# One attention layer's instruction order: a block of queries projected between the first scores, TensorE held to the written order, turned keys in two pairs and a single

## The chip, the cores and the metric

The kernel runs on one core of one Trainium2 chip. The metric is the device time of one execution in microseconds (us), as the median of several runs. A core has a matrix engine (TensorE, PE in the profile), a vector engine (VectorE, DVE), a scalar engine (ScalarE, ACT), GpSimd (POOL) and SyncE (SP), which here only issues DMAs. Each engine works through its own list of instructions in order and waits on semaphores for the others.

## The reference, cut to what matters

The program is a two-layer trunk over 512 latent tokens and 256 context tokens of width 1024. Layer 0 mixes tokens with a chunkwise mLSTM, layer 1 with windowed attention, and each layer ends with a squared-ReLU MLP. Only layer 1's attention is touched. Its core is, with 16 query heads in 4 groups of 4, one key/value head for each group, head width 64, blocks of 128 queries, a window of 128 and one sink logit for each head:

```python
rel = k_idx - SWA_BLOCK - q_idx
def block(args):
    j, qb = args                       # one block of 128 queries
    kb = lax.dynamic_slice_in_dim(kp, j * SWA_BLOCK, 3 * SWA_BLOCK, axis=1)   # its own block and both neighbours
    ...
    m = jnp.maximum(jnp.maximum(jnp.max(s_lat, -1), jnp.max(s_ctx, -1)), sink_g)
    p_lat = jnp.exp(s_lat - m[..., None])
    p_ctx = jnp.exp(s_ctx - m[..., None])
    den = jnp.sum(p_lat, -1) + jnp.sum(p_ctx, -1) + jnp.exp(sink_g - m)
    o = jnp.einsum("bhgqk,bkhd->bqhgd", p_lat, vb) + jnp.einsum("bhgqc,bchd->bqhgd", p_ctx, cv)
    return o / jnp.moveaxis(den, 3, 1)[..., None]
```

Before it stand the projections of queries, keys and values (queries and keys are rotated, "rope"), behind it an output projection of 1024 by 1024 that is added to the latent stream. In layer 1, the last one, only the latent tokens need an output.

## The kernel before, in words

**Numbers in two halves.** Most operands are held as a high half and a low half (`whi`, `wlo`, `uH`, `uL`), so that one product takes three matmuls (`mm3`, line 107). A weight comes in through `unit_begin` (line 88): a DMA on SP into `raw`, a copy to `whi` on ACT (L95), and, when its returned `end()` is called, a subtraction to `wlo` on DVE (L98). `prefetch` begins a unit and puts its `end()` into a list that `tick()` counts down, one tick for each command of the order tables.

**Names in the profile.** `pk`, `pq`, `pv` are the projections of keys, queries and values (L115, TensorE); `rt`/`rtx`, `rx` are the rotated queries or keys (L1905 to L1907); `ks` and `qs` are keys and queries stacked as high and low half (L1916 on ACT, L1917 on DVE); `s` are the scores of one head for one block of queries (L1956/L1957, or L1960/L1961); `e` are their exponentials; `pt` the transposed (turned) exponentials; `ph` the copy of `pt`; `av` the weighted values; `mm<-y` the output projection; `vst` the values.

**Scores.** `scores(g, j)` (L1932) makes the four heads of group g for query block j, and yields after each one. Blocks j=0 and j=3, at the edge, see two blocks of keys and the context, 512 columns in all, so two heads share one tile `s` of 1024 columns: head 0 with head 1 and head 2 with head 3. Their scores are two matmuls of 512 columns. Blocks j=1 and j=2 see three blocks of keys, 640 columns: one tile for each head, four matmuls. There are two such tiles. After the matmuls, one custom DVE instruction (L1964, with a read of its accumulator) adds the mask and finds the minimum, ACT takes the exponential (L1968) and the sink's (L1971), and after each second head DVE forms the reciprocal of the denominator (L1975, L1976) and POOL scales both heads (L1978). In a shared tile the second head's first matmul carries a semaphore wait on ACT, for the exponential of the first head.

**Weighing.** `weigh` (L1982) gives two lists of steps: T, "turn" (four transposes L1994, one key block of the four heads, and the copy `ph` on ACT, L1999), and V, `values` (the product with the values, L2011/L2017, and the evacuation L2019/L2022). j=0 and j=3 have 4 T steps, j=1 and j=2 have 5.

**The order.** There are 16 turns, n = 4g + j. Each turn walks through the string PAT: S is the scores of one head (running six heads ahead), T one turn step, V one values step, F one filler step. Fillers are queries of a later group (`q_steps`: 8 steps of three 512-column matmuls, then the rotation) in the turns that `qat` names, and parts of the output projection of an earlier group (`out_steps`: two steps of three 512-column matmuls for each part, then an evacuation `hL` on DVE, L1867) in the counts that `outs` names. The last turn, n=15, uses the string PL. Before turn 0 a prologue makes the first six heads' scores with the value projections of key blocks 2 and 3 as fillers (`v_steps`, four steps of six 256-column `pv` matmuls for each block): one S, then two F, six times. `need` says at which turn a weight's DMA is begun.

**Who decides in the end.** The kernel is compiled by a scheduler that may move an instruction past others on its engine. An instruction wrapped in `keep_in_program_order` keeps its place among others so wrapped. `self.matmul` (L113) wraps its matmul when `pin_mm` is set; in before it is not set in this layer, and `scores` and `weigh` call `nc.tensor.matmul` directly.

Of the kernel before, what the change touches and what calls it, by code (L numbers as in the profile page):

```python
# [14 lines left out]
AX = mybir.AxisListType  # L15


PAT = "SFTTFSFTFSTFTFSFFVVV"
PL = "FTTFVTFTFFVFF"
PSUM = bass.MemoryType.PSUM  # L20

P = 128
# [34 lines left out]
class Trunk:  # L57
# [1593 lines left out]
    def layer1_mix(self, u):  # L1651
        nc, tc, a = self.nc, self.tc, self.a
        self.ctx_ada.close()
        with tc.tile_pool(name="sw", bufs=1, reuse_waits="tile") as sw:
# [34 lines left out]
            for m in range(2):  # L1689
# [6 lines left out]
                    self.keys_out(0, rk[0](), slice(0, NL))  # L1696
                self.queries_out(sw, 0, m, rq)

            def v_steps(j, pool, tag):
                ps = pool.tile([P, 512], F32, name="pv", tag=tag)[:, :256]  # L1700
                for i in range(0, KT, 2):
                    self.values(ps, j, rows, i, i + 2)
                    if i < KT - 2:
                        yield
                put(j, ps)
                yield
            for j in range(2):
                for _ in v_steps(j, *((self.mm, "mm"), (self.at, "at"))[j]):
                    pass
            self.ctx_mm.close()  # L1710
            with tc.tile_pool(name="sc", bufs=2, space=PSUM, reuse_waits="tile") as sc, \
                    tc.tile_pool(name="pt1", bufs=3, space=PSUM, reuse_waits="tile") as pt, \
# [1 line left out]
                ys = [None] * KVH  # L1714
                todo = [(g, j) for g in range(KVH) for j in range(4)]
                parts = []
                qat = {0: (1, 0), 1: (1, 1), 2: (2, 0), 3: (2, 1), 4: (3, 0), 8: (3, 1)}
                outs = {5: 3, 6: 3, 7: 2, 9: 3, 10: 2, 11: 2, 12: 2, 13: 3, 14: 6, 15: 6}
                late, soon, units, yh = [], [], {}, {}
                need = {0: "q10", 1: "q11", 2: "q20", 3: "q21", 4: "q30", 5: "o00", 6: "o01", 8: "q31", 9: "o10", 10: "o11",  # L1720
                        12: "o20", 14: "o21 o30", 15: "o31"}
                self.units, self.yh = units, yh

                def prefetch(n, d):
# [40 lines left out]
                    for n, (g, j) in enumerate(todo):  # L1765
                        yield from self.scores(sw, g, j, sc, curs[n])
                sg = all_scores()
                fl = chain(v_steps(2, pt, "pt"), v_steps(3, pt, "pt"))
                for i in range(6):
                    next(sg)  # L1770
                    tick()
                    if i == 1:
                        prefetch(0, 2)
                    next(fl, None)
                    next(fl, None)
                for n, (g, j) in enumerate(todo):
                    if ys[g] is None:
                        ys[g] = sw.tile([P, 2, NL], F32, name=f"yT{g}", tag="yT", bufs=2)
                    if j == 0 and g:
                        parts += self.out_part(g - 1, ys, pt, "pt")  # L1780
                    if n == 14:
                        y3 = self.split_y(3)
                        st3 = {"y": y3}
                        self.st = {}
                        self.tmpA = [self.base.tile([P, NL], F32, name=f"nA{t}", tag=t) for t in ("uH5", "uL5", "uL4")]
                        pa = self.out_part(3, ys, pt, "pt", "A", st3)
                        parts = [f for i in range(4) for f in (parts[i], pa[i])] + pa[4:5]
                        self.split_half(ys[3], y3, 0)
                    if j == 0 and g:
                        yh[g - 1] = self.split_y(g - 1, ys)  # L1790
                    fl = filler(n)
                    wg = self.weigh(sw, g, j, curs[n], pt, av, ys)
                    for i, cmd in enumerate(PAT if n < 15 else PL):
                        next({"S": sg, "F": fl}.get(cmd) or wg[cmd], None)
                        tick()
                        if i == 6:
                            prefetch(n + 1, 7)
                    for it in (wg["T"], wg["V"], fl):
                        for _ in it:
                            pass  # L1800
                self.split_half(ys[3], y3, 1)
                for f in pa[5:]:
                    for _ in f():
# [23 lines left out]
    def split_y(self, g, ys=None):  # L1827

        nc = self.nc
        r = []  # L1830
        for i in range(2):
            hi, lo = [self.base.tile([P, NL], F32R, name=f"y{n}{g}{i}",
                                     tag=f"u{'HL'[n]}{(g - 2) * 6 + i}" if g > 1 else f"uC{2 * i + n}") for n in range(2)]
            if ys:
                nc.scalar.copy(out=hi, in_=ys[g][:, i, :])
                nc.vector.tensor_tensor(out=lo, in0=ys[g][:, i, :], in1=hi.bitcast(F32), op=ALU.subtract)
            r.append((hi, lo))
        return r
# [93 lines left out]
    def scores(self, sw, g, j, scp, out):  # L1932

        nc = self.nc
        d = self.swd
        mm = nc.tensor.matmul
        q4 = d["qs"][g][:, :, j * P:(j + 1) * P]
        k0, k1 = [d["ks"][:, i, g, :] for i in range(2)]
        lo, hi = max(0, j - 1), min(4, j + 2)
# [42 lines left out]
    def weigh(self, sw, g, j, ps_, ptp, avp, ys):  # L1982

        nc = self.nc
        d = self.swd
        mm = nc.tensor.matmul
        blks = list(range(max(0, j - 1), min(4, j + 2))) + [4, 5]
        pq = []

        def turn():  # L1990
            for n, kb in enumerate(blks):
                pt = ptp.tile([P, 512], F32, name="pt", tag="pt")
                for i in range(4):
                    nc.tensor.transpose(out=pt[:, i * P:(i + 1) * P], in_=ps_[i][:, n * P:(n + 1) * P],  # L1994
                                        identity=self.ident)
                self.nph = (getattr(self, "nph", 0) + 1) % 6
                pool, tag = (self.base, f"uC{4 + self.nph}") if self.nph < 4 else (sw, f"ph{self.nph}")
                ph = pool.tile([P, 512], F32, name="ph", tag=tag)
# [176 lines left out]
```

## Time and profile before

| quantity | value |
|---|---|
| median of 3 runs | 1493.35 us (1492.82 to 1493.48) |
| the profiled execution's own time | 1492.53 us |
| its span | 1490.8 us (so 1.73 us lie around it) |
| mean granted TensorE clock | 0.995 of full |
| keys and first queries of layer 1's attention | from 912.9 us |
| first score | 943.00 us |
| last weighted value | 1135.6 us |
| end of its output projection | 1141.8 us |

The profile is one execution. Start times are counted from the start of the span. A row of the timeline gives the start, the busy time, the engine, the source line, the operation, output from inputs, the shape and the count; in brackets stands the idle time ahead of it on that engine and what ended it. Matmuls are pipelined, so a matmul's cost in a dense stretch is the distance from its start to the start of the next one, not its busy time.

### The profile page before, as it was taken

Reading aid. Unit: us, or ns where it says so; the run is one execution under the profiler, and the core shown is the slowest. Engines: PE = TensorE matmul, PEld = TensorE weight load, DVE = VectorE, ACT = ScalarE, POOL = GpSimd, SP = SyncE. Lnnn points to the kernel's source line nnn. Section 1 sums busy time; section 2 is a strip of 40 time slices with the busy share of each in tenths; the row PEclk is TensorE's granted clock in tenths of the full one; section 3 lists DMA queues with packets and bytes.
Section 4 is the critical chain, followed back from the end, with each engine's and each line's share of the span. In section 5 each row is a group of like instructions: output and inputs, shape, how many; then the busy total and the mean of one; then the engine's idle time right before and its main releaser. Section 6 shows DMA issues by size and latency. Waiting matters only on the chain.

```text
span 1490.8 us, 22747 instructions
## 1 busy us (share of the span) xinstructions
PE 1470.4 (99%) x8600; PEld 1299.2 (87%) x8601; DVE 1102.8 (74%) x1996; ACT 740.1 (50%) x1492; POOL 291.5 (20%) x289
## 2 busy tenths in 40 slices
PE   9999999999999999999999999899999999999998
PEld 5888999989899999999999998776767988888886
DVE  4987648488897878788777767667777775857697
ACT  4555353553754241432414344677775655455454
POOL 0123131333103223212223121133332000000000
PEclk9999999999999999999999999999999999999999
DMA  9223313235132334343343422221111432240221
GB/s 374 86 95 123 124 57 125 93 114 166 44 113 85 133 117 146 114 155 130 126 156 100 154 71 89 68 65 57 50 43 61 180 128 98 89 138 33 95 71 57
DMA packets 49317, 161.14 MB, mean 108 GB/s; under 512 B 5776, under 2 KB 8592, under 8 KB 49080
## 3 DMA queue, kind: packets, MB, share of 16 engines
q1 hardware_dynamic: 48032, 157.92, 30.8%
q10 hardware_dynamic: 1175, 1.77, 0.3%
q8 instruction: 68, 1.11, 0.3%
q14 instruction: 42, 0.34, 0.1%
HBM read 153.90 MB, written 2.10 MB: 105 GB/s over the span
## 4 chain that ended last, share of the span: by engine, by line
PE 89%; DVE 6%; ACT 3%; issue 1%; POOL 0%; DMA 0%; POOLq 0%; ACTq 0%; DVEq 0%
PE mm L115 53%; PE p L115 10%; PE pq L115 3%; PE kept L115 3%; PE av L2011 2%; PE pt L1994 2%; PE pb L115 2%; PE pc L115 2%; PE acc L115 1%; PE at L1009 1%; PE s L1960 1%; PE at L966 1%; PE pk L115 1%; PE arow L115 1%; PE s L1961 1%
## 5 line engine op out<-in xcount | busy, mean ns | idle before, releaser
L115 PE MATMUL mm<-h,whi 128*128 128x384 f32 x1024 | 262.4, 337 | 0.0
L1054 DVE TENSOR_TENSOR wlo<-raw,whi 128x1024 fp32r<-128x1024 f32 (+2 forms) x138 | 165.2, 1201 | 74.4 <-ACT whi L1053 72.1
L1053 ACT CAST whi<-raw 128x1024 fp32r<-128x1024 f32 (+2 forms) x138 | 136.0, 991 | 141.0 <-PE mm L115 90.3
L115 PE MATMUL mm<-uH,whi 128*128 128x512 f32 (+1 forms) x496 | 186.6, 380 | 0.0
L115 PE MATMUL mm<-uH,wlo 128*128 128x512 f32 (+1 forms) x496 | 186.6, 377 | 0.0
L115 PE MATMUL mm<-uL,whi 128*128 128x512 f32 (+1 forms) x496 | 186.2, 377 | 0.0
L115 PEld LDWEIGHTS mm<-h,whi 128*128 128x128 f32 x1024 | 185.5, 188 | 0.3 <-DVE h L1054 0.2
L115 PE MATMUL mm<-h,wlo 128*128 128x384 f32 x512 | 172.0, 336 | 0.0
L282 DVE SCALAR_TENSOR_TENSOR adap<-raw,crow 128x1024 bf16<-128x1024 f32 x128 | 165.3, 1292 | 8.3 <-DMA raw<-ada 7.4
L115 PE MATMUL p<-t,whi 128*128 128x384 f32 x448 | 114.3, 336 | 0.0
L1053 ACT CAST whi<-sum 128x512 fp32r<-128x512 f32 (+1 forms) x42 | 31.8, 759 | 159.3 <-PE mm L115 81.1
L115 PEld LDWEIGHTS mm<-uH,wlo 128*128 128x128 f32 x496 | 93.4, 188 | 17.4 <-issue 0.2
L115 PEld LDWEIGHTS mm<-uL,whi 128*128 128x128 f32 x496 | 93.6, 189 | 15.4 <-DVE uL L1099 0.3
L115 PEld LDWEIGHTS mm<-uH,whi 128*128 128x128 f32 x496 | 92.7, 189 | 15.7 <-issue 0.2
L115 PEld LDWEIGHTS mm<-h,wlo 128*128 128x128 f32 x512 | 96.1, 188 | 0.0
L1054 DVE TENSOR_TENSOR wlo<-wb,whi 128x1024 fp32r<-128x1024 f32 x49 | 59.2, 1224 | 35.9 <-ACT whi L1053 35.8
L1054 DVE TENSOR_TENSOR h<-r,h 128x384 fp32r<-128x384 f32 (+2 forms) x100 | 58.2, 584 | 34.2 <-ACT h L1053 33.9
L115 PEld LDWEIGHTS p<-t,whi 128*128 128x128 f32 x448 | 81.2, 188 | 0.0
L1053 ACT CAST whi<-wb 128x1024 fp32r<-128x1024 f32 x49 | 51.5, 1052 | 57.8 <-PE mm L115 48.2
L1978 POOL TENSOR_SCALAR e<-e,den 128x512 f32<-128x512 f32 (+1 forms) x64 | 53.5, 848 | 130.3 <-DVE den L1976 98.9
L115 PE MATMUL mm<-uC,whi 128*128 128x256 f32 x416 | 77.0, 285 | 0.3 <-ACT whi L1053 0.3
L115 PE MATMUL p<-t,wlo 128*128 128x384 f32 x224 | 75.4, 337 | 0.0
(417 smaller groups left out, 3528.4 us busy)
## 6 DMA issues: line engine op xcount, KB each, us to landing
raw<-ada SPq DMA_DIRECT2D x80, 512.0 KB, 3.4
raw<-w SPq DMA_DIRECT2D x64, 512.0 KB, 3.4
raw<-w2a SPq DMA_DIRECT2D x32, 512.0 KB, 3.2
wb<-w2b SPq DMA_DIRECT2D x28, 512.0 KB, 4.1
adaw<-ada SPq DMA_DIRECT2D x16, 512.0 KB, 11.2
raw<-wqk SPq DMA_DIRECT2D x8, 512.0 KB, 4.6
raw<-wv SPq DMA_DIRECT2D x8, 512.0 KB, 3.3
raw<-wo SPq DMA_DIRECT2D x8, 512.0 KB, 3.2
```

Source lines behind the costliest of these rows:

```text
L115: i = self.nc.tensor.matmul(**kw)
L282: self.tc.keep_in_program_order(nc.vector.scalar_tensor_tensor(out=pr, in0=w, scalar=0.5, in1=self.crow[:, v, :], op0=ALU.mult, op1=ALU.mu ...
L966: mm(out=kv[d][64 * h:64 * h + 64, n * VW:(n + 1) * VW], lhsT=kp[:, d, j, 64 * h:64 * h + 64], rhs=v[:, j, h, :], start=True, stop=True)
L1009: mm(out=o[hh][:, i * VW:(i + 1) * VW], lhsT=pw[g, d, hh][:, i, :], rhs=v[:, 3 * g + i, hh, :], start=False, stop=i == 2)
L1053: keep(self.nc.scalar.copy(out=hi, in_=src))
L1054: keep((eng or self.nc.vector).tensor_tensor(out=lo, in0=src, in1=hi.bitcast(F32), op=ALU.subtract))
L1960: mm(out=o, lhsT=ql, rhs=k0[:, cs], start=True, stop=False)
L1961: mm(out=o, lhsT=ql, rhs=k1[:, cs], start=False, stop=True)
L1978: nc.gpsimd.tensor_scalar(out=out[ii][:, :W], in0=out[ii][:, :W], scalar1=den[:, ii:ii + 1], scalar2=1.0, op0=ALU.mult, op1=ALU.mult)
L1994: nc.tensor.transpose(out=pt[:, i * P:(i + 1) * P], in_=ps_[i][:, n * P:(n + 1) * P], identity=self.ident)
L2011: mm(out=o[i * DH:(i + 1) * DH, :], lhsT=v(n + i), rhs=pq[n + i], start=n == 0, stop=n == len(blks) - 2)
```

## The change

Five edits, all in layer 1's attention.

1. The first weight block of group 1's queries (`q10`) is begun before the value projections and split into halves after the first of them; its projection becomes a filler of the prologue. The blocks after it move up by one turn in `qat`: (1,1) in turn 0, (2,0) in 1, (2,1) in 2, (3,0) in 3, (3,1) in 4; turn 8 has none any more.
2. The prologue follows a new string PS: `SSFFSSFFFFSFFFSFFFFF`.
3. `pin_mm` is set from the prologue to the end of turn 15, `scores` and `weigh` call `self.matmul`, and the transposes are wrapped, so TensorE keeps the written order.
4. PAT has the T steps as pair, pair, single. Turns 5 to 12 use a new string PO with four F steps, and `outs` is evened out to two parts in each.
5. `split_y` puts the halves of y of groups 1 and 2 into other tiles; `need` moves the output weights' DMAs.

```diff
-PAT = "SFTTFSFTFSTFTFSFFVVV"
+PAT = "SFTTFSFFSFTTFSTFFVVV"
+PO = "STTFSFSTTFSTFVVV"
+PS = "SSFFSSFFFFSFFFSFFFFF"
 PL = "FTTFVTFTFFVFF"
...
+            first = self.unit_begin(a["wsq"][1, 0])
...
             for j in range(2):
                 for _ in v_steps(j, *((self.mm, "mm"), (self.at, "at"))[j]):
                     pass
+                if j == 0:
+                    first[2]()
...
-                qat = {0: (1, 0), 1: (1, 1), 2: (2, 0), 3: (2, 1), 4: (3, 0), 8: (3, 1)}
-                outs = {5: 3, 6: 3, 7: 2, 9: 3, 10: 2, 11: 2, 12: 2, 13: 3, 14: 6, 15: 6}
-                late, soon, units, yh = [], [], {}, {}
...
+                qat = {0: (1, 1), 1: (2, 0), 2: (2, 1), 3: (3, 0), 4: (3, 1)}
+                outs = {**{n: 2 for n in range(5, 13)}, 13: 4, 14: 6, 15: 6}
+                late, soon, units, yh = [], [], {"q10": first}, {}
...
-                fl = chain(v_steps(2, pt, "pt"), v_steps(3, pt, "pt"))
-                for i in range(6):
-                    next(sg)
+                fl = chain(v_steps(2, pt, "pt"), v_steps(3, pt, "pt"), q_steps(1, 0))
+                self.pin_mm = True
+                for i, cmd in enumerate(PS):
+                    next(sg if cmd == "S" else fl, None)
                     tick()
-                    if i == 1:
-                        prefetch(0, 2)
-                    next(fl, None)
-                    next(fl, None)
+                    if i == 8:
+                        prefetch(0, 8)
+                for _ in fl:
+                    pass
...
-                    for i, cmd in enumerate(PAT if n < 15 else PL):
+                    for i, cmd in enumerate(PO if 4 < n < 13 else PAT if n < 15 else PL):
...
+                self.pin_mm = False
...
-                                     tag=f"u{'HL'[n]}{(g - 2) * 6 + i}" if g > 1 else f"uC{2 * i + n}") for n in range(2)]
+                                     tag=f"u{'HL'[n]}{(0, 2, 0, 6)[g] + i}" if g else f"uC{2 * i + n}") for n in range(2)]
...
-        mm = nc.tensor.matmul
+        mm = self.matmul
...
-                    nc.tensor.transpose(out=pt[:, i * P:(i + 1) * P], in_=ps_[i][:, n * P:(n + 1) * P],
-                                        identity=self.ident)
+                    self.tc.keep_in_program_order(nc.tensor.transpose(
+                        out=pt[:, i * P:(i + 1) * P], in_=ps_[i][:, n * P:(n + 1) * P], identity=self.ident))
```

Three places show what this moves in the compiled programs. Lines of the changed kernel are two to eight higher, and its matmuls all carry the line of `self.matmul`, L117. What an instruction waits for stands in brackets.

**The first scores, TensorE.** In the program before, `s_9816` is the tile of heads 0 and 1, `s_9864` that of heads 2 and 3, and `pv_9823`, `pv_9871` are the value projections of key blocks 2 and 3:

```order
L115 MATMUL pv_9823<-whi_9353,uL0_9038 128x256
L1956 MATMUL s_9816<-ks_9560,qs_9699 128x512 [waits DVE_49]
L115 MATMUL pv_9823<-whi_9353,uH1_9039 128x256
...
L1957 MATMUL s_9816<-ks_9560,qs_9699 128x512 [waits DMAHW5_49,DMAHW7_49,DMAHW4_49,DMAHW3_49]
L115 MATMUL pv_9823<-whi_9393,uL5_9048 128x256
...
L1956 MATMUL s_9864<-ks_9560,qs_9699 128x512 [waits DVE_49,PE_49]
...
L115 MATMUL pq_9943<-uL0_9038,whi_9848 128x512
L1956 MATMUL s_9816<-ks_9560,qs_9699 128x512 [waits Activation_49]
```

In the changed program the tile of heads 0 and 1 is `s_9822`, that of heads 2 and 3 `s_9852`, and `pv_9839` is the value projection of key block 2:

```order
L117 MATMUL pv_9782<-whi_9393,uL7_9052 128x256
L117 MATMUL s_9822<-ks_9560,qs_9699 128x512 [waits DVE_49]
L117 MATMUL s_9822<-ks_9560,qs_9699 128x512 [waits DMAHW5_49,DMAHW7_49,DMAHW4_49,DMAHW3_49]
L117 MATMUL s_9822<-ks_9560,qs_9699 128x512 [waits Activation_49]
L117 MATMUL pv_9839<-whi_9353,uH0_9037 128x256
...
L117 MATMUL pv_9839<-whi_9353,uL3_9044 128x256
L117 MATMUL s_9852<-ks_9560,qs_9699 128x512 [waits DVE_49,PE_49]
L117 MATMUL s_9852<-ks_9560,qs_9699 128x512
L117 MATMUL s_9852<-ks_9560,qs_9699 128x512 [waits Activation_49]
```

Before, the scheduler put the scores of head 2 and 45 matmuls of the value projections between the scores of heads 0 and 1; now the two heads of a tile stand directly behind each other, with the second one's wait for ACT in between, and the value projections stand behind them.

**The first mask instruction, VectorE.** Before, the last rotation and stacking of group 0's keys and queries (`ks`, `qs`) is followed by the mask instructions (ISA) of heads 0 and 1:

```order
L1907 TENSOR_TENSOR rtx_9738<-rtx_9738 128x512 [waits DVE_49]
L1917 TENSOR_TENSOR ks_9560<-rt_9650,ks_9560 64x512 [waits Activation_49] x2
L1917 TENSOR_TENSOR qs_9699<-rtx_9738,qs_9699 64x512 [waits Activation_49] x2
L1964 ISA s_9816,nb_9814<-s_9816,msk_9552,nsink_9550 128x512 [waits PE_49,Pool_49]
L1964 ISA nb_9814 128x1
```

Now the low half of `q10`'s weight stands ahead of the first mask instruction:

```order
L1915 TENSOR_TENSOR rtx_9738<-rtx_9738 128x512 [waits DVE_49]
L1925 TENSOR_TENSOR ks_9560<-rt_9650,ks_9560 64x512 [waits Activation_49] x2
L1925 TENSOR_TENSOR qs_9699<-rtx_9738,qs_9699 64x512 [waits Activation_49] x2
L100 TENSOR_TENSOR wlo_9753<-raw_9750,whi_9752 128x1024
L1972 ISA s_9822,nb_9820<-s_9822,msk_9552,nsink_9550 128x512 [waits PE_49,Pool_49]
```

One instruction moved in: before, `q10`'s `wlo` stood behind the fifth mask instruction of the prologue.

**Turn 5, TensorE.** The end of the turn before, with the scores of heads of group 1, block 3 (512 columns), turned keys, output projection and weighted values:

```order
L1994 MATMUL pt<-ident,e 128x128 x4
L115 MATMUL mm<-y_10448,whi 128x512
L115 MATMUL mm<-y_10449,whi 128x512
L115 MATMUL mm<-y_10448,wlo 128x512
L2011 MATMUL av<-ph,vst_9561 64x512
L1956 MATMUL s<-ks,qs 128x512
L1957 MATMUL s<-ks,qs 128x512
L2011 MATMUL av<-ph,vst_9562 64x512
```

And the same place now, from the first score of such a pair to the second:

```order
L117 MATMUL s<-ks,qs 128x512 [waits PE_49,Activation_49]
L117 MATMUL s<-ks,qs 128x512
L2002 MATMUL pt<-ident,e 128x128 [waits PE_49]
L2002 MATMUL pt<-ident,e 128x128 x3
L117 MATMUL mm<-y_10489,whi 128x512 [waits DVE_49]
L117 MATMUL mm<-y_10490,whi 128x512
L117 MATMUL mm<-y_10489,wlo 128x512
L117 MATMUL s<-ks,qs 128x512 [waits Activation_49]
```

Before, the scheduler had put the second score in between the weighted values; now it stands ahead of them, behind two turn steps and one filler step, and the weighted values stand together.

More of the change, by code (lines that the diff above doesn't have):

```diff
@@ L1716, in layer1_mix @@
                 parts = []
-                qat = {0: (1, 0), 1: (1, 1), 2: (2, 0), 3: (2, 1), 4: (3, 0), 8: (3, 1)}
-                outs = {5: 3, 6: 3, 7: 2, 9: 3, 10: 2, 11: 2, 12: 2, 13: 3, 14: 6, 15: 6}
-                late, soon, units, yh = [], [], {}, {}
-                need = {0: "q10", 1: "q11", 2: "q20", 3: "q21", 4: "q30", 5: "o00", 6: "o01", 8: "q31", 9: "o10", 10: "o11",
-                        12: "o20", 14: "o21 o30", 15: "o31"}
+                qat = {0: (1, 1), 1: (2, 0), 2: (2, 1), 3: (3, 0), 4: (3, 1)}
+                outs = {**{n: 2 for n in range(5, 13)}, 13: 4, 14: 6, 15: 6}
+                late, soon, units, yh = [], [], {"q10": first}, {}
+                need = {0: "q11", 1: "q20", 2: "q21", 3: "q30", 4: "q31", 5: "o00", 7: "o01", 9: "o10", 11: "o11", 13: "o20",
+                        14: "o21 o30", 15: "o31"}
                 self.units, self.yh = units, yh
@@ L1985, in weigh @@
         d = self.swd
-        mm = nc.tensor.matmul
+        mm = self.matmul
         blks = list(range(max(0, j - 1), min(4, j + 2))) + [4, 5]
```

## The prediction

> **What bounds the kernel now.** I read the page first: the span, the share of each engine, the chain that ended last.
>
> ```profile
> span 1490.8 us, 22747 instructions
> PE 1470.4 (99%) x8600; PEld 1299.2 (87%) x8601; DVE 1102.8 (74%) x1996; ACT 740.1 (50%) x1492; POOL 291.5 (20%) x289
> PE 89%; DVE 6%; ACT 3%; issue 1%; POOL 0%; DMA 0%; POOLq 0%; ACTq 0%; DVEq 0%
> ```
>
> TensorE is the bound. No matmul is taken away, so the change can win only what TensorE loses in this layer, and lose what it adds. Next I asked for windows, and for TensorE's waits from 943 us to 1140 us.
>
> ```profile
> 943.00:968.00 25.00, 20.29 (x110) 16.44 (x111) 15.36 (x34) 14.96 (x38) 5.10 (x6) 0.86 0.15 43
> 990.00:1010.00 20.00, 20.00 (x108) 14.33 (x107) 14.34 (x33) 15.83 (x36) 7.77 (x10) 1.00 0.17 50
> PE s L1960 <- ACT e L1968: 3.7, 2, 1.8
> PE mm L115 <- ACT ph L1999: 0.3, 1, 0.3
> ```
>
> The columns are busy us of PE, PEld, DVE, ACT, POOL, then clock, DMA share and GB/s. The first scores have TensorE idle for 4.7 us and at 0.86 of its clock; the turns behind them are full. So the prologue decides, and in the turns only gaps too small for a busy share. Its TensorE timeline:
>
> ```profile
> 941.35 0.28 PE L115 MATMUL pv<-whi,uL 128*128 128x256 f32 x1
> 943.00 0.50 PE L1956 MATMUL s<-ks,qs 128*128 128x512 f32 x1 [1.37 <-DVE rtx L1905]
> 949.75 0.28 PE L115 MATMUL pv<-whi,uL 128*128 128x256 f32 x1
> 949.87 0.40 PE L115 MATMUL pq<-uH,whi 128*128 128x512 f32 x1
> 950.11 0.40 PE L115 MATMUL pq<-uL,whi 128*128 128x512 f32 x1
> 950.74 0.40 PE L1957 MATMUL s<-ks,qs 128*128 128x512 f32 x1
> 952.97 0.39 PE L1960 MATMUL s<-ks,qs 128*128 128x256 f32 x1 [1.83 <-ACT e L1968]
> 955.42 0.78 PE L1956 MATMUL s<-ks,qs 128*128 128x512 f32 x1
> 958.46 0.58 PE L1960 MATMUL s<-ks,qs 128*128 128x256 f32 x1 [1.83 <-ACT e L1968]
> 961.87 0.48 PE L115 MATMUL pq<-uH,whi 128*128 128x512 f32 x1
> 965.17 0.28 PE L1960 MATMUL s<-ks,qs 128*128 128x256 f32 x1
> 965.76 0.60 PE L1994 MATMUL pt<-ident,e 128*128 128x128 f32 x4
> 966.12 0.48 PE L115 MATMUL pq<-uH,whi 128*128 128x512 f32 x1
> ```
>
> From start to start a 256-column matmul costs 0.12 us (949.75 to 949.87), one of 512 columns 0.23 (949.87 to 950.11), a head of four score matmuls 0.59 (965.17 to 965.76), a turn step of four transposes 0.36 plus what its neighbour pays, which I count as 0.44. Between 941.47 and 961.87 stand 45 `pv`, 3 `pq`, 8 wide score matmuls, 3 heads of four and 8 transposes: 5.4 + 0.7 + 1.8 + 1.8 + 0.9 = 10.6 us of work in 20.4 us. **Before loses 9.8 us here.** Some of it is clock, in windows of 3.4 us:
>
> ```profile
> 941.33:944.74 3.41, 2.04 (x16) 1.00 0.44 118
> 951.57:954.98 3.41, 1.28 (x6) 1.00 0.00 0
> 954.98:958.40 3.42, 1.54 (x4) 0.50 0.00 0
> 958.40:961.80 3.40, 3.34 (x12) 0.50 0.20 57
> ```
>
> Here the columns are PE busy, clock, DMA. A window that was 1.28 or 1.54 busy is followed by one at half clock, a window that was 2.04 busy is not, and after a full one (958.40) the clock is back.
>
> **Part by part. The prologue (edits 1, 2, 3).** What comes before the first score is unchanged on TensorE and VectorE, so that score stays at 943.0, but three `pv` fewer stand ahead (941.1). Its second matmul waits for a DMA of keys, which I put at 943.9. Then, in the written order, TensorE stands at head 1, which waits for head 0's exponential, and all `pv` and `pq` are queued behind it. What that waits for:
>
> ```profile
> 946.35 1.41 DVE L1917 TENSOR_TENSOR qs<-rtx,qs 64x512 fp32r<-64x512 f32 x2
> 947.78 0.76 DVE L1964 CUSTOM_DVE_ANT_0 s<-s,msk,nsink 128x512 f32<-128x512 f32 x1
> 951.29 0.76 DVE L1964 CUSTOM_DVE_ANT_0 s<-s,msk,nsink 128x512 f32<-128x512 f32 x1 [2.69 <-PE s L1957]
> 952.14 0.69 ACT L1968 ACTIVATE e<-s,nb 128x512 f32<-128x512 f32 x1 [1.34 <-DVE nb L1964]
> 958.90 1.21 DVE L98 TENSOR_TENSOR wlo<-raw,whi 128x1024 fp32r<-128x1024 f32 x1
> ```
>
> VectorE rotates and stacks until 947.76, then makes `q10`'s `wlo`, 1.21 us, to 948.97, and only then masks. From a mask's start to the score behind its exponential it is 951.29 to 952.97, 1.68 us. So head 1 starts at 950.65. TensorE stood from 944.3: **6.3 us in one piece**; before it filled this with the 45 `pv`.
>
> By the windows, 944.74 to 948.15 is empty and 948.15 to 951.57 a quarter full, so it is half clock until 954.98. There head 1 and twelve `pv` cost 2 x 0.46 + 2 x 1.44 = 3.8 us: to 954.5, then head 2 (0.8, partly at half clock) to 955.3. From head 2's second matmul, about 954.9, to the next score of its tile is 950.74 to 952.97, 2.23 us: head 3 at 957.1, idle 1.8 us. Behind it stand 24 `pv`, a head, 12 `pv`, 3 `pq`, a head, 21 `pq`, with no wait that I can see. Losses: 1.9 ahead of the first score, 0.7 inside it, 6.3, half clock 2.4, then 1.8 = 13.1 to 13.2 us. **Against 9.8: +3.4 us.** Bounds: without half clock the 2.4 shrink, and the wait for head 2 moves up, to +1.5; if the window 954.98 to 958.40, which I get at about half full (between 1.54 and 2.04), drops the clock again, 1.7 us more, +5.1.
>
> [...]
>
> **The turns 0 to 4.** The same matmuls with T steps in pairs. Transposes cost the same in pairs as alone, `q10`'s block moved into the prologue, and each later block moves up a turn with its DMA on SP, its `whi`, `wlo`, its rotation with four DMAs and its sum on POOL. In 990 to 1010 us DVE (14.3 of 20), ACT (15.8) and POOL (7.8) have room, and TensorE has no gap: nothing either way. Were that cover gone, one `wlo` of 1.21 us could stand ahead of a mask.
>
> **The turns 5 to 12.** What goes are values blocks that the scheduler split with a score:
>
> ```profile
> 1027.77 1.07 PE L2011 MATMUL av<-ph,vst 128*64 128x512 f32 x2
> 1032.30 0.63 PE L115 MATMUL mm<-y,whi 128*128 128x512 f32 x2
> 1039.72 0.39 PE L1956 MATMUL s<-ks,qs 128*128 128x512 f32 x1
> 1043.13 0.63 PE L115 MATMUL mm<-y,whi 128*128 128x512 f32 x2
> ```
>
> Split (turn 5), a values block with two scores takes 4.53 us (1027.77 to 1032.30), whole (turn 6) 3.41: 1.1 us each, three times in these turns (near 1027, 1071, 1082), 3.3 us. Beside them I count 2.4 us of gaps of about 0.1. What comes is PO: between two heads of one tile stand two T and one F, 0.87 + 0.69 us, where PAT had another F, 0.69.
>
> ```profile
> 1036.86 0.39 PE L1956 MATMUL s<-ks,qs 128*128 128x512 f32 x1
> 1037.06 0.75 DVE L1867 SCALAR_TENSOR_TENSOR hL<-mm,mod,hL 128x512 f32<-128x512 f32 x1 [0.81 <-PE mm L115]
> 1037.79 0.75 DVE L1964 CUSTOM_DVE_ANT_0 s<-s,msk,nsink 128x512 f32<-128x512 f32 x1
> 1038.02 0.59 ACT L1999 COPY ph<-pt 128x512 f32<-128x512 f32 x1 [0.30 <-PE pt L1994]
> 1038.70 0.69 ACT L1968 ACTIVATE e<-s,nb 128x512 f32<-128x512 f32 x1
> ```
>
> Undisturbed, from a head's start to the next of its tile takes 2.23 + 0.23 = 2.46 us; PO offers 0.46 + 0.87 + 0.69 = 2.02. So a pair at the start of a turn (four of them) waits 0.4. A pair in the middle has an `hL` ahead of its mask and two `ph` copies around its exponential, as here, where the exponential ends at 1039.39, 2.67 us after the head's start with one copy; with two, 0.59 more, I take 3.1: 1.1 us of wait, four times. Two turns (8 and 12) have `split_y`'s casts on ACT ahead of the exponential; I take 0.5 each, about one `ph` copy. Sum 1.6 + 4.4 + 1.0 = 7.0 us against 5.7 that go, the 0.1 gaps taken as swallowed by the waits: **+1.3 us**. Bounds: no wait at all, -4.5 with some small gaps kept; all waits and all small gaps, +3.7.
>
> **The turns 13 to 15.** The split at turn 14, 1.1, and the wait of 0.3 for `ph` go: **-1.3 us**. Everything behind is TensorE's and shifts as a whole.
>
> Sum: 3.4 + 0 + 1.3 - 1.3 = +3.4 us. The profiled execution took 1492.53 us and would take 1495.9; the median, 1493.35, is 0.8 above it, so 1496.7.
>
> **The rivals.** (R1) The other side: the exponential's wait does not hold head 1 as I read it (it is satisfied early, as a count and not an event of head 0). Then TensorE flows through the prologue from 943.9, the turns begin 7.7 us sooner, minus the first exponentials' delay of some 3.4 us: -4.3, 1489.0. It decides if head 1 starts before the first mask has run. Against it: before, too, 952.97 and 958.46 started 0.14 us behind an exponential. (R2) The waits in turns 5 to 12 hide as before, since queues on ACT and VectorE shift with TensorE: C is -4.5, net -2.4, 1490.9. For it: before shows almost no wait on exponentials there; against it, the gap is 0.69 us shorter. (R3) A second spell of half clock in the prologue: +5.1, 1498.4. For it, the row of 1.54; against it, that of 2.04. [...] It keeps its chance, as the rows above let short gaps throttle. That the change does less than it says (the transposes pinned, the pairs formed) is not open: the compiled order shows it.
>
> **How the numbers follow.** Forecast 0.55 (own range +1.5 to +5.5), R1 0.10, R2 0.17, R3 0.18. The range leaves out R1 and a tip above R3: 1490.5 to 1499.5. A change of 0.2% is 3.0 us, about what a measurement of this kernel can tell from none. Faster: R1 and 0.04 of R2, 0.14. Within: the rest of R2 and 0.25 of the forecast's lower part, 0.38. Slower: 0.30 of the forecast and R3, 0.48.
>
> **What would show it.** In the changed profile: a wait of head 1 on `e` of about 6 us near 944 to 951, the first mask near 949, clock 0.50 from 948 to 955, head 3 waiting about 1.8 us, the last prologue `pq` near 968.6; in turns 5 to 12 `s <- ACT e` waits that sum to about 7 us; no values block split. The prediction is wrong if head 1 starts before 949, or if those waits sum to under 4 us.

## The result and the profile after

The changed kernel takes 1508.22 us (median of 4, 1505.23 to 1509.08) against 1493.41 us (median of 4): the ratio is 1.0096, 95% interval 1.0079 to 1.0114. It is slower by 14.8 us. The forecast was slower by 3.4, at most 6.

The page of the changed kernel, its span, engines and the chain that ended last:

```profile
span 1506.9 us, 22753 instructions
PE 1471.2 (98%) x8600; PEld 1300.3 (86%) x8601; DVE 1100.8 (73%) x1996; ACT 741.3 (49%) x1492; POOL 296.4 (20%) x289
PE 83%; DVE 8%; ACT 5%; issue 2%; DMA 1%; POOL 1%; ACTq 0%; SPq 0%; POOLq 0%; DVEq 0%
```

TensorE is as busy as before (1471.2 and 1470.4 us) in a span that is 16.1 us longer, and on the chain its share falls from 89% to 83%, with VectorE and ScalarE in its place. The added time is TensorE standing. The windows of the changed kernel (busy us of PE, PEld, DVE, ACT, POOL, then clock, DMA share, GB/s) say where:

```profile
943.00:968.00 25.00, 14.95 (x83) 12.83 (x82) 13.96 (x28) 13.01 (x30) 2.73 (x4) 0.80 0.23 63
990.00:1010.00 20.00, 17.59 (x91) 11.52 (x90) 11.56 (x26) 14.83 (x35) 7.45 (x9) 1.00 0.13 41
1030.00:1050.00 20.00, 18.00 (x95) 11.46 (x93) 14.69 (x33) 17.56 (x42) 9.33 (x9) 1.00 0.13 40
```

The prologue is emptier (14.95 of 25 where before had 20.29), and the turns, full before (20.00 of 20), now have holes of 2 us and more in each 20. TensorE's waits in the changed kernel from 942 us to 1158 us:

```profile
PE s L117 <- ACT e L1976: 14.6, 15, 6.2
PE pt L2002 <- ACT ph L2007: 2.4, 2, 1.2
PE mm L117 <- DVE hL L1875: 1.8, 2, 0.9
PE s L117 <- DVE rtx L1913: 1.7, 1, 1.7
PE pq L117 <- DVE wlo L100: 1.0, 2, 0.6
```

The columns are the sum in us, the number, the longest. The first and the fourth row were forecast; the second, third and fifth were not.

To compare kernels whose work is moved, I take TensorE's loss in a stretch: the time from its first matmul to the first behind it, less the dense cost of every matmul in it, as it stands from start to start in the profiles of before and of the changed kernel (0.231 us for 512 columns, 0.175 for 384, 0.12 for 256, 0.109 for a transpose; of the weighted values 0.215 and 0.13). The stretches run from the last key projection to the last weighted value of turns 4 and 12, and to the end of the layer's output projection. "Start" is the first key projection of layer 1. All values are of the one profiled execution of each kernel, in us.

| kernel | start | prologue and turns 0 to 4 | turns 5 to 12 | turns 13 to 15 | time of that execution |
|---|---|---|---|---|---|
| before | 913.05 | 11.4 | 7.8 | 3.4 | 1492.53 |
| changed | 915.68 | 19.7 | 13.8 | 3.1 | 1508.65 |
| e1 changed, not held | 913.00 | 8.1 | 11.5 | 5.6 | 1494.62 |
| e2 before, held | 913.19 | 14.9 | 6.5 | 2.7 | 1494.22 |
| e3 changed, prologue free | 913.24 | 13.1 | 13.3 | 3.1 | 1499.15 |
| e4 changed, wide gap | 913.49 | 18.9 | 12.6 | 3.8 | 1505.18 |
| e5 changed, old PAT | 915.60 | 15.1 | 15.8 | 2.7 | 1505.86 |
| e6 changed, stack later | 914.46 | 18.2 | 18.1 | 3.1 | 1510.25 |
| e7 changed, spread prologue | 913.81 | 12.7 | 13.7 | 3.1 | 1499.69 |
| e8 changed, wlo later | 913.94 | 20.3 | 13.3 | 3.1 | 1507.07 |
| e9 changed, mended | 913.00 | 8.7 | 15.7 | 2.7 | 1496.83 |
| e10 before, turns held | 913.93 | 12.0 | 6.6 | 2.7 | 1492.13 |
| e11 changed again | 915.28 | 19.3 | 13.7 | 3.1 | 1507.79 |
| e12 mended, parts in reserve | 913.41 | 8.7 | 9.6 | 2.5 | 1490.96 |

Time less start less losses is 556.4 to 556.9 us in every row, so at most some 0.5 us is not accounted for. Of the 16.1 us between the first two executions, 8.3 are lost in the prologue and turns 0 to 4, 5.9 in turns 5 to 12, 0.3 are won in 13 to 15 (the sum is 0.4 too high, that rest), and 2.6 lie ahead of layer 1, where no instruction was changed. There the changed kernel's execution had more half clock (a granted clock of 0.50) than before's in two places, near 40 us (a mean of 0.50 from 36 to 42 us, in before 0.72) and near 398 us. Matmul by matmul it falls behind by some 1.5 us at each, and wins 0.4 us back elsewhere. The second one, windows of the changed kernel:

```profile
396.00:399.00 3.00, 2.98 (x19) 2.90 (x20) 2.62 (x4) 1.35 (x2) 1.53 (x1) 0.77 0.33 116
399.00:402.00 3.00, 3.00 (x20) 3.00 (x19) 0.10 (x1) 0.51 (x2) 0.51 (x1) 0.66 0.71 229
```

and before:

```profile
396.00:399.00 3.00, 3.00 (x27) 3.00 (x27) 1.50 (x3) 0.42 (x2) 2.04 (x1) 1.00 0.62 188
399.00:402.00 3.00, 3.00 (x28) 3.00 (x26) 2.60 (x5) 2.46 (x6) 0.00 (x0) 1.00 0.49 169
```

This stretch of layer 0 runs at 0.77 and 0.66 of the clock in the one and at full clock in the other.

### The profile page after: what moved, and what is told of

It is laid out like the page before. It is cut to its first block, busy times and chain, and to the rows that moved or that the text cites. A ratio compares the mean times of both kernels' runs of the same rounds, so it can differ in the third digit from the quotient of the medians.

```text
span 1506.9 us, 22753 instructions
## 1 busy us (share of the span) xinstructions
PE 1471.2 (98%) x8600; PEld 1300.3 (86%) x8601; DVE 1100.8 (73%) x1996; ACT 741.3 (49%) x1492; POOL 296.4 (20%) x289
## 4 chain that ended last, share of the span: by engine, by line
PE 83%; DVE 8%; ACT 5%; issue 2%; DMA 1%; POOL 1%; ACTq 0%; SPq 0%; POOLq 0%; DVEq 0%
PE mm L117 52%; PE p L117 10%; PE kept L117 3%; PE pb L117 2%; PE pc L117 2%; PE av L117 2%; PE s L117 2%; PE acc L117 1%; PE at L1011 1%; ACT e L1976 1%; PE pq L117 1%; PE pt L2002 1%; DVE s L1972 1%; PE arow L117 1%; PE at L968 1%
## 5 line engine op out<-in xcount | busy, mean ns | idle before, releaser
L117 PE MATMUL mm<-h,whi 128*128 128x384 f32 x1024 | 262.4, 337 | 0.0
L117 PE MATMUL mm<-uH,whi 128*128 128x512 f32 (+1 forms) x496 | 186.5, 380 | 0.0
L117 PE MATMUL mm<-uH,wlo 128*128 128x512 f32 (+1 forms) x496 | 186.5, 377 | 0.0
L117 PE MATMUL mm<-uL,whi 128*128 128x512 f32 (+1 forms) x496 | 186.3, 377 | 0.0
L117 PEld LDWEIGHTS mm<-h,whi 128*128 128x128 f32 x1024 | 185.4, 188 | 0.3 <-DVE h L1056 0.2
L117 PE MATMUL mm<-h,wlo 128*128 128x384 f32 x512 | 172.0, 336 | 0.0
L117 PE MATMUL p<-t,whi 128*128 128x384 f32 x448 | 114.3, 336 | 0.0
L117 PEld LDWEIGHTS mm<-uH,wlo 128*128 128x128 f32 x496 | 93.4, 188 | 17.3 <-issue 0.2
L117 PEld LDWEIGHTS mm<-uL,whi 128*128 128x128 f32 x496 | 93.5, 189 | 15.4 <-DVE uL L1101 0.3
L117 PEld LDWEIGHTS mm<-uH,whi 128*128 128x128 f32 x496 | 92.7, 189 | 15.8 <-issue 0.2
L117 PEld LDWEIGHTS mm<-h,wlo 128*128 128x128 f32 x512 | 96.1, 188 | 0.0
L1986 POOL TENSOR_SCALAR e<-e,den 128x512 f32<-128x512 f32 (+1 forms) x64 | 58.7, 928 | 138.5 <-DVE den L1984 110.7
L117 PEld LDWEIGHTS p<-t,whi 128*128 128x128 f32 x448 | 81.3, 188 | 0.0
L1055 ACT CAST whi<-wb 128x1024 fp32r<-128x1024 f32 x49 | 51.6, 1054 | 57.8 <-PE mm L117 48.2
L117 PE MATMUL mm<-uC,whi 128*128 128x256 f32 x416 | 78.4, 288 | 0.3 <-ACT whi L1055 0.3
L117 PE MATMUL p<-t,wlo 128*128 128x384 f32 x224 | 75.4, 337 | 0.0
## 6 DMA issues: line engine op xcount, KB each, us to landing
adaw<-ada SPq DMA_DIRECT2D x16, 512.0 KB, 11.2
```

What stands on the lines that cost most here:

```text
L117: i = self.nc.tensor.matmul(**kw)
L1055: keep(self.nc.scalar.copy(out=hi, in_=src))
L1986: nc.gpsimd.tensor_scalar(out=out[ii][:, :W], in0=out[ii][:, :W], scalar1=den[:, ii:ii + 1], scalar2=1.0, op0=ALU.mult, op1=ALU.mult)
```

## The experiments

**Held or not, old strings or new.** Theory A: TensorE held to the written order stands at waits that it used to fill with later work. Theory B: the new strings (PS, PAT, PO) set the waits, held or not. Three kernels separate them, a fourth the gap in PO.

e1 takes the holding out of the changed kernel:

```diff
-                self.pin_mm = True
                 for i, cmd in enumerate(PS):
...
-                    self.tc.keep_in_program_order(nc.tensor.transpose(
-                        out=pt[:, i * P:(i + 1) * P], in_=ps_[i][:, n * P:(n + 1) * P], identity=self.ident))
+                    nc.tensor.transpose(out=pt[:, i * P:(i + 1) * P], in_=ps_[i][:, n * P:(n + 1) * P],
+                                        identity=self.ident)
```

> The changed kernel with all its tables, but neither matmuls nor transposes of this layer are held to the written order. Theory A (TensorE held in order stands at waits that it used to fill with later work): the losses in the prologue and in turns 0 to 4 go, 3 and 5 us, those in turns 5 to 12 shrink by half or more: 1493 to 1497 us. Theory B (the new strings set the waits, held or not): the pairs with a short gap still wait, 1500 us or more.

Measured: 1495.33 us, ratio 1.0011 (1.0001 to 1.0020). Of some 14 us only 1.6 are left. The prologue and turns 0 to 4 now lose 3.3 us less than before (8.1 against 11.4). That may be `q10`'s block in the prologue, placed by the scheduler; the new strings came with it, and this execution's mean granted clock is 0.998, before's 0.995, so this run alone doesn't show which. Turns 5 to 12 still lose 3.7 us more than before; the scheduler splits values blocks again there (turns 6, 7, 8, 11 and 12). So A holds for the prologue, and B for a part of the turns.

e2 puts the holding into the kernel before, from the prologue to the end of turn 15 (`pin_mm`, `self.matmul`, the transposes wrapped), with its old strings and tables.

> The kernel before with its old tables, with matmuls and transposes of this layer held to the written order. Theory A: TensorE stands in the prologue (about 6 us at head 1, part of it made up by fewer later waits) and in the turns: 3 to 9 us above before, 1496 to 1502 us. Theory B: the old strings have room for the chain, only the splits of the values go: 1489 to 1494 us.

Measured: 1495.02 us, ratio 1.0009 (1.0000 to 1.0019), between the two expectations. The prologue and turns 0 to 4 lose 3.5 us more than before, but turns 5 to 12 lose 1.3 less, and 13 to 15 0.7 less. Its waits on exponentials are three:

```profile
PE s L115 <- ACT e L1970: 6.8, 3, 2.8
```

The changed kernel has fifteen. With old strings, holding the order costs nothing in the turns; it wins the splits. Theory A is wrong for the turns and right for the prologue.

e3 is the changed kernel with `self.pin_mm = True` moved from ahead of the prologue to ahead of turn 0.

> The changed kernel with TensorE held to the written order only from turn 0 on, so that the prologue is free. Theory A: the wait of 6 us at head 1 is gone and with it 3 to 5 us: 1503 to 1505 us against 1508; turns 0 to 15 as in the changed kernel. Theory B: the prologue's loss comes from the early low half of the weight on VectorE, so 1 us at most is won.

Measured: 1500.61 us, ratio 1.0048 (1.0032 to 1.0065), 5.4 us under the changed kernel's second measurement (e11, below) and 7.6 under its first. By losses it is 6.6 us (19.7 to 13.1): 5.6 up to the end of turn 0, where head 1's stand is gone, and 1.0 in turn 4. That is more than the 3 to 5 that theory A gave, and the time lies below its range. The stands at `pt` in turns 1 and 2 are there as in the changed kernel.

e4 widens the gap between the heads of a tile in turns 5 to 12:

```diff
-PO = "STTFSFSTTFSTFVVV"
+PO = "SFTTFSSFTTFSTVVV"
```

> The changed kernel with the string of turns 5 to 12 changed to SFTTFSSFTTFSTVVV: the two heads of a tile are two T and two F steps apart, as before, and the two middle heads stand side by side; the count of F steps is the same. If the short gap of PO sets the waits there: their sum of some 7 us falls to 2 or less, 1502 to 1504 us. If the waits come from what is queued on ScalarE and VectorE, they stay within 1.5 us: 1506 to 1509 us.

Measured: 1505.31 us, ratio 1.0076 (1.0061 to 1.0091); turns 5 to 12 lose 12.6 us instead of 13.8. The time lies between the two expectations; the losses, which shrink by 1.2 us, speak for the queues on ScalarE and VectorE. The losses of turns 6 and 10, with two pairs each, fell from 2.2 and 2.1 us to 0.7, and other waits took their place, in e4's timeline:

```profile
1043.97 0.65 PE L117 MATMUL av<-ph,vst 128*64 128x256 f32 x4 [1.26 <-ACT ph L2007]
1070.89 0.85 PE L117 MATMUL s<-ks,qs 128*128 128x256 f32 x4 [0.87 <-ACT e L1976]
1075.47 0.50 PE L117 MATMUL mm<-y,wlo 128*128 128x512 f32 x1 [0.63 <-DVE wlo L100]
1102.58 0.86 PE L117 MATMUL s<-ks,qs 128*128 128x256 f32 x4 [1.35 <-ACT e L1976]
```

Two ways of putting four filler steps into a turn were tried, PO and this one, and with both some later step meets a chain on ScalarE or VectorE.

**Why turns 0 to 4 stand.** They should have cost nothing. The changed kernel, turn 1, on TensorE and then on ScalarE:

```profile
992.84 0.66 PE L2002 MATMUL pt<-ident,e 128*128 128x128 f32 x4 [1.21 <-ACT ph L2007]
```

```profile
989.12 1.05 ACT L97 CAST whi<-raw 128x1024 fp32r<-128x1024 f32 x1
990.07 0.68 ACT L1976 ACTIVATE e<-s,nb 128x512 f32<-128x512 f32 x1
990.93 1.24 ACT L1924 CAST qs<-rt 64x512 fp32r<-64x512 f32 x2
992.20 1.08 ACT L2007 COPY ph<-pt 128x512 f32<-128x512 f32 x2
```

There are three `pt` buffers. The block of queries keeps one through its eight steps, a pair of T takes the other two, and the single T behind it needs the first `ph` copy. That copy stands on ScalarE behind a weight's cast, an exponential and the stacking of queries.

e5 puts the old string into turns 0 to 4, 13 and 14:

```diff
-PAT = "SFTTFSFFSFTTFSTFFVVV"
+PAT = "SFTTFSFTFSTFTFSFFVVV"
```

> The changed kernel with the old string PAT (SFTTFSFTFSTFTFSFFVVV) in turns 0 to 4, 13 and 14; PO, PS, the tables and the held order stay. Theory A' (with TensorE held, the strings decide: pairs of T need two of the three pt buffers while a block of queries keeps the third, and stand until ScalarE has copied one): the 5 us that turns 0 to 4 lose more than before fall to 1 or less, 1503 to 1504.5 us against 1508. Rival C (the queries' blocks moved up by one turn are the cause: their weights and stacks come too late): nothing changes, 1507 to 1509 us.

Measured: 1504.18 us, ratio 1.0068 (1.0051 to 1.0085). Turns 0 to 4 lose 2.3 us instead of 6.9 (the prologue keeps its 12.8), as theory A' said, and rival C falls. Turn 5 loses 2.0 more than it did: the exponential that it waits for comes later, and behind this emptier window of 3.4 us the next one runs at half clock (after the comma PE busy and count, clock, DMA share, GB/s).

```profile
1038.85 0.86 PE L117 MATMUL s<-ks,qs 128*128 128x512 f32 x2 [1.94 <-ACT e L1976]
1035.88:1039.30 3.42, 1.48 (x9) 1.00 0.08 31
1039.30:1042.71 3.41, 3.41 (x13) 0.50 0.00 0
```

e6 issues the stacking later:

```diff
-                        soon.append([6, lambda g=g, b=b, x=x: self.queries_out(sw, g, b, x, self.tc.keep_in_program_order)])
+                        soon.append([13, lambda g=g, b=b, x=x: self.queries_out(sw, g, b, x, self.tc.keep_in_program_order)])
```

> The changed kernel with the stacking of rotated queries (two qs casts on ScalarE, two subtractions on VectorE) issued 13 commands after the rotation instead of 6, behind the second pair of T. If the qs casts ahead of the ph copies make TensorE wait 1.2 us for pt in turns 1 and 2, these two waits go: 2 to 3 us less, 1505 to 1506.5 us. If the pair of T alone does it, the waits stay and the time too.

Measured: 1509.79 us, ratio 1.0107 (1.0092 to 1.0122), where 1505 to 1506.5 was expected. Both waits for `pt` are gone, so the casts ahead of the copies were what held them. But the casts now stand ahead of exponentials; those waits grow from 14.6 to 18.2 us. Turn 5 alone has this one; its two matmuls are busy 1.22 us, as long as the two at 953.22 in the changed kernel, where the granted clock was 0.50:

```profile
1038.80 1.22 PE L117 MATMUL s<-ks,qs 128*128 128x512 f32 x2 [2.00 <-ACT e L1976]
```

The cause was hit, the remedy was not: moving 1.24 us of ScalarE work within the fixed order only changed who waited for it.

**The prologue.** e7 spreads the scores:

```diff
-PS = "SSFFSSFFFFSFFFSFFFFF"
+PS = "SFFFFFFFFSSFFFSFFSFFSF"
```

> The changed kernel with the prologue's string PS = SFFFFFFFFSSFFFSFFSFFSF: the same six heads and sixteen filler steps, TensorE held, but eight filler steps between heads 0 and 1 and three between heads 2 and 3. If head 1's wait for the exponential is what the prologue loses, 48 pv fill it: the wait of 6.2 us falls under 1, the half clock goes, 7 to 9 us less, 1499 to 1501 us. If the loss comes from VectorE being late for every later head, 1.5 us at most is won.

Measured: 1498.99 us, ratio 1.0037 (1.0023 to 1.0050). The prologue loses 5.8 us instead of 12.8; of the half clock one window is left, 945.76 to 949.18, where a `pv` takes 0.21 us from start to start and not 0.12. In e7's timeline head 1 (the first two of the four matmuls at 952.22) waits no more, head 3 still waits 1.52:

```profile
944.67 0.47 PE L117 MATMUL s<-ks,qs 128*128 128x512 f32 x1 [0.40 <-DMA ks<-ks]
952.22 1.09 PE L117 MATMUL s<-ks,qs 128*128 128x512 f32 x4
956.90 0.73 PE L117 MATMUL s<-ks,qs 128*128 128x512 f32 x2 [1.52 <-ACT e L1976]
```

e8 makes the weight's low half later, by moving `first[2]()` from the value projections into the prologue's loop, at `i == 1`.

> The changed kernel with the low half of the first query weight of group 1 made behind the masks of heads 0 and 1 instead of ahead of them. The prediction priced this instruction at 1.21 us ahead of the first mask: head 1's wait falls from 6.2 to 5.0 us, the time by 1 to 2 us. If that instruction is hidden, nothing changes.

Measured: 1506.68 us, ratio 1.0088 (1.0073 to 1.0103). Head 1's wait falls from 6.2 to 5.1 us, as priced. The time doesn't settle it: it is 1.5 us under the changed kernel's first measurement and 0.6 above its second (e11). In the profiled execution the prologue even loses 14.5 us, 1.7 more, because the clock stays at half for 17.1 us, until 962.72, on through the window with the second, short wait; the changed kernel's was at half for 10.2 us. As head 1's wait is 1.1 us shorter, the longer half clock costs some 2.8 us. The spells of half clock up to the end of the attention last 3.41 and 6.83 us in before's profile, 6.83, 3.41 and 10.24 in the changed kernel's, and e8's in the prologue 17.07: one, two, three and five times 3.41 us. They lie elsewhere in each execution. e8 in windows of that length, cut where its spell ends (PE busy and count, clock, DMA share, GB/s):

```profile
949.06:952.48 3.42, 2.11 (x8) 0.50 0.25 81
952.48:955.89 3.41, 2.52 (x10) 0.50 0.00 0
955.89:959.30 3.41, 2.58 (x10) 0.50 0.45 154
959.30:962.72 3.42, 3.42 (x18) 0.50 0.00 0
962.72:966.13 3.41, 3.41 (x26) 1.00 0.00 0
```

The changed kernel:

```profile
943.77:947.18 3.41, 1.12 (x4) 1.00 0.50 132
950.59:954.01 3.42, 0.79 (x2) 0.50 0.71 217
954.01:957.42 3.41, 3.41 (x15) 0.50 0.07 28
957.42:960.83 3.41, 1.69 (x11) 1.00 0.00 0
960.83:964.25 3.42, 3.42 (x30) 1.00 0.00 0
```

In the changed kernel a full window, 954.01 to 957.42, fell between the two waits, and behind it the clock was back. In e8 the work between the waits, 950.37 to 955.0, was shared by two windows that were each partly empty.

**A version that keeps the idea.** e9 is the changed kernel with TensorE held, e7's PS, `first[2]()` at `i == 0`, the old PAT in all turns up to 14, and `outs = {5: 3, 6: 3, 7: 2, 8: 1, 9: 3, 10: 3, 11: 1, 12: 1, 13: 3, 14: 6, 15: 6}` with the output weights begun to match.

> The changed kernel with TensorE held, q10 in the prologue, and the places that stood mended: PS = SFFFFFFFFSSFFFSFFSFFSF, the low half of the first weight behind the mask of head 0, the old PAT in turns 0 to 14 and no PO, and the parts of the output projection put where two heads of a tile follow each other in the middle of a turn (three in turns 5, 6, 9, 10, 13; one in 8, 11, 12; two in 7). If the stands found so far are the whole cause, the losses are about 5 us in the prologue, 2 in turns 0 to 4, 6.5 in 5 to 12, 3 in 13 to 15, 16 to 17 us against 22.7 of before: 1487 to 1489 us. If the moved queries' blocks cost something of their own, 1491 us or more.

Measured: 1497.65 us, ratio 1.0027 (1.0016 to 1.0037). The prologue and turns 0 to 4 came out at 8.7 us, where some 7 had been added up; turns 5 to 12 are far off, at 15.7 instead of 6.5. Turns 8 and 12 alone lose 5.4 and 6.7, at these waits and with a window of half clock behind each (from 1056.71, where eight transposes at 1056.98 are busy 1.91 us and those at 1066.99 are busy 1.04, and from 1101.08), in e9's timeline:

```profile
1055.43 0.50 PE L117 MATMUL mm<-y,whi 128*128 128x512 f32 x1 [1.52 <-ACT y L1843]
1099.26 0.50 PE L117 MATMUL mm<-y,whi 128*128 128x512 f32 x1 [2.76 <-ACT y L1843]
```

My table let the first filler step of these turns use the halves of y of a group that had just ended. The changed kernel keeps two parts of the group before for these turns; that part of its design was sound, and I had undone it. e12 keeps one:

```diff
-                outs = {5: 3, 6: 3, 7: 2, 8: 1, 9: 3, 10: 3, 11: 1, 12: 1, 13: 3, 14: 6, 15: 6}
+                outs = {5: 3, 6: 3, 7: 1, 8: 1, 9: 3, 10: 3, 11: 1, 12: 1, 13: 4, 14: 6, 15: 6}
```

> The kernel of the run before with one part of the output projection of the last group but one kept for turns 8 and 12 (outs 5: 3, 6: 3, 7: 1, 8: 1, 9: 3, 10: 3, 11: 1, 12: 1, 13: 4), so that no part there needs the halves of y that have just been begun. If the 5.4 and 6.7 us that turns 8 and 12 lost were this wait alone, they fall to 1 or 2 each and the time to 1488 to 1491 us, below before. If the turns with few filler steps stand anyway, 1493 us or more.

Measured: 1491.17 us, ratio 0.9987 (0.9978 to 0.9996): faster than before by 0.13%, and just above the 1488 to 1491 expected. Turns 8 and 12 lose 2.6 each, more than the 1 or 2 expected, without half clock (eight transposes stay at 1.03 to 1.04 us from 1054 to 1104 us, and the mean granted clock is 0.996, e9's 0.994); two waits of 1.52 us for exponentials are left there.

e10 takes the smallest part of the change that could win: the kernel before, held from turn 0 only.

> The kernel before with its old tables and a free prologue, TensorE held to the written order only from turn 0 on. Theory A' (held order costs nothing in the turns where the old strings leave room): prologue as before, turns 5 to 15 lose 2 us less than before since the values are not split: 1490.5 to 1492.5 us. If holding the order costs in the turns: 1494 us or more.

Measured: 1492.13 us, ratio 0.9990 (0.9981 to 0.9999). Turns 5 to 15 lose 1.9 us less than before (9.3 against 11.2), as expected; the difference is at the edge of what can be measured.

**The spread.** e11 is the changed kernel unedited.

> The changed kernel once more, unedited, for its spread: its first profile was 2.6 us late before the layer's first instruction. If that is chance of the execution, some executions lie near 1505.5 us and their profiles start layer 1 near 913 us; if the change does it, all lie near 1508 us.

Measured: 1506.04 us, ratio 1.0081 (1.0067 to 1.0095), with executions at 1504.49, 1504.82, 1507.26 and 1507.79: two pairs 2.8 us apart in one program. Its profile (1507.79) starts layer 1 at 915.28. So some 3 us come and go with the execution. Whether they are the 2.6 us ahead of layer 1 is not shown directly, as the two quick executions were not profiled; their mean granted clock, 0.995 where the two late ones have 0.992 and 0.993, fits it. The profiles of e5 and e6 start layer 1 late too, at 915.60 and 914.46, with mean granted clocks of 0.992 and 0.993. The kernel before also has a spread (1492.17 to 1496.22 in these runs). What picks the half clock in layer 0 wasn't tried.

## Why the prediction was wrong, point by point

**The prologue was right** in mechanism, and its sum was close. Less the 2.64 us that the first score is late, the changed kernel's rows are 943.0, 943.9, 950.58, 954.15 and 956.79, where the prediction had 943.0, 943.9, 950.65, 954.5 and 957.1:

```profile
945.64 0.50 PE L117 MATMUL s<-ks,qs 128*128 128x512 f32 x1 [1.73 <-DVE rtx L1913]
946.54 0.47 PE L117 MATMUL s<-ks,qs 128*128 128x512 f32 x1 [0.40 <-DMA ks<-ks]
953.22 1.22 PE L117 MATMUL s<-ks,qs 128*128 128x512 f32 x2 [6.21 <-ACT e L1976]
956.79 0.92 PE L117 MATMUL s<-ks,qs 128*128 128x512 f32 x2
959.43 0.73 PE L117 MATMUL s<-ks,qs 128*128 128x512 f32 x2 [1.72 <-ACT e L1976]
```

On VectorE the weight's low half stood where the compiled order put it:

```profile
950.40 1.23 DVE L100 TENSOR_TENSOR wlo<-raw,whi 128x1024 fp32r<-128x1024 f32 x1
951.54 0.75 DVE L1972 CUSTOM_DVE_ANT_0 s<-s,msk,nsink 128x512 f32<-128x512 f32 x1
```

The loss up to the end of `q10` is 12.8 us against 9.8: +3.0 where +3.4 was said. Its parts are 1.9, 0.7, 6.4, half clock 1.9 and 2.0 us, where the prediction had 1.9, 0.7, 6.3, 2.4 and 1.8. That the half clock ended about where it was said, at 954.78 less the shift where 954.98 was said, is partly luck: the prediction took the clock's windows from before's execution, and they lie elsewhere in each (before's spell ended at 961.80, the changed kernel's at 957.42, e8's at 962.72). e7 shows the cause by filling the wait.

**The step that failed is "The turns 0 to 4 ... nothing either way".** They cost +5.3 us: the prologue and these turns lose 8.3 more, of which 3.0 are the prologue's. Counted with the slower first matmul behind each, two stands at `pt` of 1.43 each, two at `wlo` of 0.69 and 0.87 and one at an exponential of 0.64 add up to 5.1. The step argued from busy shares of a stretch that a free scheduler had arranged. It named one thing that could come ahead of a mask and missed what the order showed: of three `pt` buffers one is held by the queries, so a pair of T makes the next T wait for a copy on ScalarE. e5 (turns 0 to 4 at 2.3) and e6 (no wait for `pt`) show it: it takes both the pair and the casts ahead of the copy. The two stands at `wlo` went in e5 and e6 as well; why they came isn't shown.

**Turns 5 to 12 were mis-sized:** +5.9 measured, +1.3 said, +3.7 the upper bound. The idle time itself came out nearly as summed, 7.2 us against 7.0. Eleven waits for exponentials make 5.4 us: at the start of a turn 0.27 to 0.40 (said 0.4), at a pair in the middle 0.76 to 0.97 (said 1.1), in turns 8 and 12 0.15 each (said 0.5), and one of 0.47 in turn 5 that was not listed. Two more, 1.8 us, are at something else not listed, an output part in turns 8 and 12 that needs a `pt` buffer which VectorE must empty first:

```profile
1074.08 0.72 PE L117 MATMUL mm<-y,whi 128*128 128x512 f32 x2 [0.89 <-DVE hL L1875]
1096.10 0.73 PE L117 MATMUL s<-ks,qs 128*128 128x512 f32 x2 [0.96 <-ACT e L1976]
```

The term that failed is what a stand costs. The second row waited 0.96, and the matmul ahead of it and its own first one took 1.69 us from start to start, where two dense ones take 0.46: 1.23 us lost. The thirteen stands lose 10.7 us, 3.5 more than their idle time. The prediction had not used this although before showed it: its one wait of 0.33 for `ph` lost 0.60. What went, splits and small gaps, is then 4.7 us and not 5.7; the small gaps that I took as swallowed are partly still there.

The prediction's 2.67 us from a head's start to the end of its exponential is 2.53 by its rows, 1036.86 to 1039.39. With the 0.14 us to the next score it is 2.67, so its sum stands.

**Turns 13 to 15** won 0.3 us, not 1.3: the splits went, but a score at 1136 us waits 0.9 for an exponential.

**The rivals.** R1 fell: head 1 waited 6.21 us. R2 fell: the waits did not hide. R3, more half clock in the prologue, did not come in the changed kernel's profile: the window with the second wait, 957.42 to 960.83, was used for 1.69 us and was followed by full clock. e8 has more of it, at some 2.8 us where 1.7 had been priced for one window. Windows of 3.41 us in the attention, by the busy time that the profile gives TensorE: at full clock those used for 1.12 us (changed), 1.28 (before), 1.48 (e5) and 1.59 (e7) were followed by half clock, and none used for 1.69 or more in before and in the changed kernel was. Two of e7's, where no wait is over 1.73 us:

```profile
942.35:945.76 3.41, 1.59 (x9) 1.00 0.38 105
945.76:949.18 3.42, 3.42 (x18) 0.50 0.41 89
```

At half clock windows used for 0.00 and 0.79 us (changed), 1.54 (before) and 2.11, 2.52 and 2.58 (e8) were followed by half clock again, and those used for 3.34 (before), 3.41 (changed) and 3.42 (e8) by full clock. So the changed kernel, with 1.69, missed R3 narrowly by these rows.

**What the range left out** was that the turns 0 to 4, 5 to 12 and 13 to 15 could all be wrong the same way: by 5.3, 4.6 and 1.0 us. The 2.6 us ahead of layer 1 came on top. In the turns gaps were looked for where the old order had them. Neither sign that was named for a wrong prediction came: head 1 started behind 949 us, and the waits in turns 5 to 12 sum to 5.4 us. Both watch steps that held; none was set for turns 0 to 4.

## What to carry to other kernels

When an order that a scheduler chose is replaced by one that is written and held, each step of the new order has to be priced for itself: its buffer, its queue on the other engines, its releaser. A busy share of the old order says nothing about it. Holding the order cost nothing in turns 5 to 15 where the strings left room for the chain behind each score (e10), and some 6 to 7 us where two dependent heads stood next to each other (e3, e7). A queue's work moved to another place of a fixed order moved the wait and didn't remove it (e6: the 2.4 us at `pt` went, those at exponentials grew from 14.6 to 18.2); filler work put into the wait removed it (e7: head 1's 6.21 us went).

## What the runs showed of the hardware that was not expected

The same program differed by 2.8 us from one execution to the next (e11), with a lower mean granted clock in the late ones (0.992 and 0.993 against 0.995): in the changed kernel's profile half clock fell on dense matmuls of layer 0, from 35.82 us behind a full window without a wait and from 397.63 behind waits of 0.33 and 0.18 us, at places where nothing had been changed. What was seen in the attention, full clock lost only behind windows used for 1.59 us or less, doesn't cover it: the window ahead of the half clock near 398 us was used for 2.88, that ahead of the one near 40 us for 3.41.

```profile
32.41:35.82 3.41, 3.41 (x39) 1.00 1.03 412
35.82:39.23 3.41, 3.41 (x14) 0.50 1.04 413
394.22:397.63 3.41, 2.88 (x22) 1.00 0.01 2
```

For changes of a few us the losses of the profiled execution, stretch by stretch, told more than the medians.

Once at half clock in the attention, TensorE got full clock back behind a fuller window in these rows: one used for 2.58 of 3.41 us was followed by half clock in e8, one used for 3.34 of 3.40 by full clock in before (958.40 to 961.80).

TensorE's stop and restart cost 0.22 to 0.27 us on top of the idle time that the waits list (1.23 for a wait of 0.96 and 1.43 for a wait of 1.21 in the changed kernel, 0.60 for one of 0.33 in before).
